# Suffix sums of a stick-breaking attention: matmuls by a matrix of ones, or a reversed scan and transposes, with two heads interleaved

## The chip, the cores and the metric

The kernel runs on one core of one Trainium2 chip. The metric is the device time of one execution in microseconds; the time before is the median of three runs.

## What is computed

The program is a two-block network on 512 tokens of width 2048. The change touches the stick-breaking attention of the first block, 12 heads of 64 columns, handled as 6 pairs. With z the scores of a head, each weight is the sigmoid of its own score times the product of one minus the sigmoids of all later keys that the query may see:

```python
z = jnp.einsum('bhqd,bhkd->bhqk', q[:, :, q0:kend], k[:, :, :kend])
causal = jnp.arange(kend)[None, :] < (q0 + jnp.arange(SB_BLOCK))[:, None]
log_1m = jnp.where(causal, jax.nn.log_sigmoid(-z), 0.0)
after = lax.cumsum(log_1m, axis=3, reverse=True) - log_1m
w = jnp.where(causal, jnp.exp(jax.nn.log_sigmoid(z) + after), 0.0)
outs.append(jnp.einsum('bhqk,bhkd->bhqd', w, v[:, :, :kend]))
```

## The kernel before

The program is one stream of dense projections with everything else laid beside it. A dense product of f32 accuracy takes three matmuls for each 128x128 tile of weights (lines 311 to 313: high parts of weight and activation, then the two cross terms); these three are one **step**. 16 steps make one projection of 128 output columns. The weights arrive in chunks of four tiles (`wr`) and are split by `split_w`: a rounded copy `wh`, written by ScalarE (line 181) or by GpSimd (line 280), and the rest `wl`, subtracted by VectorE (line 163). Which engine copies is counted: in the first pair of heads (`where` 1) GpSimd takes each, in the later pairs (`where` 2) every second one. The split of a chunk is recorded at the second step of a chunk, some three chunks ahead of its use, and each chunk has one of four buffers.

Every engine runs its instructions in the order in which the program records them; nothing is reordered later. So where a helper is recorded sets what stands behind what in each queue. `pump(n)` records the next n steps of the stream. In the attention stage, `Kern.stick`, the stream of pair j is the front of pair j+1: the projections for q, k, v and the gate, 64 steps. Beside the steps it brings at fixed places: the head norms of q and k (`head_rs`: 8 small matmuls at line 383, a Newton iteration for the root on VectorE in `newton`, two broadcast copies at line 392; the matmuls of line 383 stand behind step 41 of a pair, behind step 33 in the first pair since 8 steps are pumped ahead there), 8 transposes at line 406 some steps later, and 4 transposes of v at line 1767 behind step 55. In the first and the last pair of the stage, parts of the pooling group stand in the queues as well. `pump` also draws on a second generator, the parameters of the later S5 layer (small VectorE and GpSimd operations, written out to memory as `s5w`), at .5 of a step's pace in this stage.

One pair runs so before. For each head: 8 score matmuls (line 752, keys on partitions), then on ScalarE abs of the three banks, exp of minus that, and Ln of one plus that (lines 176 and 178, with a table load between), which gives the common part of both log sigmoids in `sbl`. Steps are pumped. VectorE then makes both log sigmoids from scores and `sbl` (lines 1824 and 1825), masks the one that is summed, and splits it into `sbh` and `sbo`. Then for each head the sums over later keys are 20 matmuls against matrices of ones (line 1846), VectorE subtracts them from `sbe`, ScalarE takes the exp, and VectorE masks the weights. The product with v (`values`, line 1791) of a pair is recorded in the next pair. Of the 64 steps, 57 are pumped among these; the rest run in a plain loop at the pair's end. In the last pair the stream is the start of the output projection (`out_ahead`).

Of the kernel before, what the change touches and what calls it, by code (L numbers as in the profile page):

```python
# [9 lines left out]
F32 = mybir.dt.float32  # L10
F32R = mybir.dt.float32r
I32 = mybir.dt.int32
BF16 = mybir.dt.bfloat16
AF = mybir.ActivationFunctionType
OP = mybir.AluOpType
# [4 lines left out]
QOFF = (512, 1024, 640, 0)  # L20
KOFF = (0, 512, 1024, 896)
BANK = ((0, 512), (512, 512), (1024, 256))
# [7 lines left out]
STICK_WAIT = (8,6)  # L30
HEAD_LAG = (3,5,7)
RWKV_STEPS = (0,0,0,(13,6),4,4,3,3,3,1,1)
STICK_STEPS = ((7,7),(9,7),(4,8),(4,11))
EVEN_STEPS = ((3,8),(6,8),10)
ODD_STEPS = ((4,20),16)
LAST_STEPS = ((4,16),14)
# [105 lines left out]
class Kern:  # L142
# [49 lines left out]
    def constants(self, tmp):  # L192
        nc, c = self.nc, self.const
        jp = tmp.tile([128, 128], I32, name="jp")
        nc.gpsimd.iota(jp, pattern=[[1, 128]], base=0, channel_multiplier=-1)
        mk = lambda name: c.tile([128, 128], F32, name=name)
# [23 lines left out]
        mr = lambda name: c.tile([128, 128], F32R, name=name)  # L220
# [3 lines left out]
        V = nc.vector  # L224
# [4 lines left out]
        self.copy(self.ident_r, self.ident)  # L229
        self.one = c.tile([128, 1], F32, name="one")  # L230
        nc.vector.memset(self.one, 1.0)
        self.ones_r = mr("ones_r")
        self.copy(self.ones_r, self.one.to_broadcast([128, 128]))

        self.suf_r = c.tile([128, 128], F32R, name="suf_r")
        nc.vector.tensor_scalar(self.suf_r, jp, 0.0, None, op0=OP.is_lt)

        self.omu = c.tile([128, 25], F32, name="omu")
        o, w = _PV["mu_a"]
        nc.vector.tensor_scalar(self.omu, self.pvt[:, o:o + w], -1.0, 1.0, op0=OP.mult, op1=OP.add)  # L240
        o, w = _PV["k_a"]
# [3 lines left out]
        for n in ("k_a", "a0", "w0", "b_glu_2"):  # L245
            o, w = _PV[n]
# [99 lines left out]

    def pump(self, n):

        for _ in range(n):
            next(self.stream, None)  # L350
            next(self.tail, None)
            self.count += EXTRA_RATE[self.where]
            if self.count >= 1:
                self.count -= 1
                next(self.extra, None)

    def big(self):
        return self.ps.tile([128, 512], F32, name="big", bufs=2)
# [1015 lines left out]
    def rwkv(self, pool, tm, yd, acts, rs):  # L1374
# [105 lines left out]
        for j in range(6):  # L1480
# [4 lines left out]
            if j:  # L1485
                pump(GRAM_WAIT)
# [286 lines left out]

    def causal(self, t):

        d = t.rearrange("p (b n) -> p b n", n=256)[:, 0::2, 0:128]
        self.mul(d, d, self.m_lt[:, None, :].to_broadcast([128, 3, 128]))
        self.mul(t[:, 896:1024], t[:, 896:1024], self.m_lt)

    def stick(self, pool, tm, yd, acts, rs, yl):  # L1780
        nc = self.nc
        V = nc.vector
        OFF = KOFF

        def values(j, vt, W, gate):
            o = self.small()
            for b in range(4):
                n = 512 - 128 * b
                for p in (0, 1):
                    h = slice(64 * p, 64 * p + 64)  # L1790
                    nc.tensor.matmul(o[h, 128 * b:512], vt[:, b, h], W[p][:, OFF[b]:OFF[b] + n],
                                     start=(b == 0), stop=(b == 3))
            self.mul(gate, o, gate)
            if j < 5:
                self.nc.sync.dma_start(yd[SB_AT[j]], gate)

        last = None
        self.second_parts(pool)
        for j in range(6):
            pools = self.pools(6 + j, pool, tm, yd, acts, rs)  # L1800
            self.stream = chain(self.stick_front(tm, j + 1, acts, rs, pool), *pools) if j < 5 else chain(
                *pools, self.out_ahead("w_out", *self.out_operands(yl, yd)))
            q, k, vt, gate = self.ready.pop(j)
            if j == 0:
                q, k = self.stacked_q(pool, q), self.stacked_k(pool, k)
                self.pump(FIRST_STEPS)
            sums = []
            self.where = 2 if j else 1
            for p in (0, 1):
                z = [self.small() for _ in range(3)]  # L1810
                at = lambda b: (z[OFF[b] // 512], OFF[b] % 512)
                for b in (0, 1, 3, 2):
                    t, o = at(b)
                    self.scores(t[:, o:o + 512 - 128 * b], p, slice(128 * b, 512), slice(128 * b, 128 * b + 128), q, k,
                                True)
                N = L = pool.tile([128, 1280], F32, name="sbl", bufs=1)
                E = pool.tile([128, 1280], F32, name="sbe", bufs=3)
                for (o, n), t in zip(BANK, z):
                    self.act(L[:, o:o + n], t[:, 0:n], AF.Abs)
                self.act(L, L, AF.Exp, scale=-1.0)  # L1820
                self.act(L, L, AF.Ln, bias=1.0)
                self.pump(STICK_STEPS[p][0])
                for (o, n), t in zip(BANK, z):
                    V.scalar_tensor_tensor(E[:, o:o + n], t[:, 0:n], 0.0, L[:, o:o + n], op0=OP.min, op1=OP.subtract)
                    V.scalar_tensor_tensor(N[:, o:o + n], t[:, 0:n], 0.0, L[:, o:o + n], op0=OP.max,
                                           op1=OP.add)
                self.causal(N)
                hi = pool.tile([128, 1280], F32R, name="sbh", bufs=2)
                lo = pool.tile([128, 1280], F32R, name="sbo", bufs=2)
                self.split(hi, lo, N)  # L1830
                sums.append((E, hi, lo))
                if last and p == 0:
                    values(*last)
                self.pump(STICK_STEPS[p][1])
            for p, (E, hi, lo) in enumerate(sums):
                s = [self.small() for _ in range(3)]
                for b in (0, 1, 3, 2):
                    t, o = s[OFF[b] // 512], OFF[b] % 512
                    mm = []
                    for b2 in range(b, 4):  # L1840
                        n = 512 - 128 * b2
                        for x in (hi, lo):
                            mm.append((t[:, o + 128 * (b2 - b):o + 128 * (b2 - b) + n],
                                       self.suf_r if b2 == b else self.ones_r, x[:, OFF[b2]:OFF[b2] + n]))
                    for i, (o_, l_, r_) in enumerate(mm):
                        nc.tensor.matmul(o_, l_, r_, start=(i == 0), stop=(i == len(mm) - 1))
                for (o, n), t in zip(BANK, s):
                    self.sub(E[:, o:o + n], E[:, o:o + n], t[:, 0:n])
                self.act(E, E, AF.Exp)
                self.pump(STICK_STEPS[2 + p][0])  # L1850
                self.causal(E)
                self.pump(STICK_STEPS[2 + p][1])
            last = j, vt, [E for E, _, _ in sums], gate
            self.where = 3
            if j == 5:
                self.where = 0
                values(*last)
                self.out_last(gate, "w_out")
            for _ in self.stream:
                pass  # L1860


# [72 lines left out]
```

## Time and profile before

| | |
|---|---|
| median of 3 runs | 3011.6 us (3009.29 to 3014.44) |
| profiled execution, its own time | 3016.27 us |
| its span | 3014.0 us |
| mean granted TensorE clock | 0.98 |
| TensorE busy | 2944.0 us, 98% |
| VectorE busy | 1619.1 us, 54% |
| ScalarE busy | 1146.2 us, 38% |
| GpSimd busy | 373.5 us, 12% |
| attention stage, first score matmul to the end of the last pair | about 602 to 973 us |

TensorE is busy nearly throughout, so what TensorE executes and the few places where it stands idle add up to the time. The other engines' shares are means over the program; what matters of them is whether a result is there when TensorE reaches the instruction that reads it.

### The profile page before, as it was taken

Reading aid. Unit: us, or ns where it says so; the run is one execution under the profiler, and the core shown is the slowest. Engines: PE = TensorE matmul, PEld = TensorE weight load, DVE = VectorE, ACT = ScalarE, POOL = GpSimd, SP = SyncE. Lnnn points to the kernel's source line nnn. Section 1 sums busy time; section 2 is a strip of 40 time slices with the busy share of each in tenths; the row PEclk is TensorE's granted clock in tenths of the full one; section 3 lists DMA queues with packets and bytes.
Section 4 is the critical chain, followed back from the end, with each engine's and each line's share of the span. In section 5 each row is a group of like instructions: output and inputs, shape, how many; then the busy total and the mean of one; then the engine's idle time right before and its main releaser. Section 6 shows DMA issues by size and latency. Waiting matters only on the chain. (4 is left out here: it accounts for less than half of the span.)

```text
span 3014.0 us, 42793 instructions
## 1 busy us (share of the span) xinstructions
PE 2944.0 (98%) x16068; PEld 2418.0 (80%) x16068; DVE 1619.1 (54%) x3253; ACT 1146.2 (38%) x2062; POOL 373.5 (12%) x819
## 2 busy tenths in 40 slices
PE   8999999999999999999999999999999999999998
PEld 6777777778887887788888887888888888888887
DVE  6655555477767675555454455354444444444534
ACT  5443443354454223223344454233333232333432
POOL 0111111013764000211100000001101010100001
PEclk9998999999999999999999999999999999999999
DMA  4211111222234555454433325543332333223443
GB/s 156 67 56 59 57 57 59 78 81 85 94 96 158 158 182 180 135 159 157 138 105 104 102 85 177 146 130 109 101 105 96 98 96 96 95 91 95 148 121 119
DMA packets 195296, 334.01 MB, mean 111 GB/s; under 512 B 29696, under 2 KB 44672, under 8 KB 193936
## 3 DMA queue, kind: packets, MB, share of 16 engines
q1 hardware_dynamic: 193808, 327.08, 34.9%
q0 software_dynamic: 1280, 4.20, 0.4%
q8 instruction: 126, 2.06, 0.3%
q14 instruction: 82, 0.67, 0.1%
HBM read 289.55 MB, written 42.70 MB: 110 GB/s over the span
## 5 line engine op out<-in xcount | busy, mean ns | idle before, releaser
L311 PE MATMUL big<-hi,wh 128*128 128x512 f32 x3424 | 1375.5, 402 | 4.6 <-ACT hi L181 3.9
L312 PE MATMUL big<-lo,wh 128*128 128x512 f32 x3424 | 1347.5, 394 | 2.3 <-DVE lo L163 2.3
L313 PE MATMUL big<-hi,wl 128*128 128x512 f32 x3424 | 1347.0, 393 | 0.7 <-DVE wl L163 0.6
L163 DVE TENSOR_TENSOR wl<-wr,wh 128x512 fp32r<-128x512 f32 x884 | 621.9, 714 | 709.9 <-ACT wh L181 707.6
L311 PEld LDWEIGHTS big<-hi,wh 128*128 128x128 f32 x3424 | 650.1, 190 | 150.2 <-issue 11.1
L181 ACT ACTIVATE wh<-wr 128x512 fp32r<-128x512 f32 x835 | 515.6, 626 | 657.1 <-PE big L312 520.2
L313 PEld LDWEIGHTS big<-hi,wl 128*128 128x128 f32 x3424 | 649.6, 190 | 141.2 <-DVE wl L163 2.7
L312 PEld LDWEIGHTS big<-lo,wh 128*128 128x128 f32 x3424 | 650.8, 190 | 132.8 <-DVE lo L163 5.6
L683 ACT ACTIVATE pm<-pm,mx 128x128 f32<-128x128 f32 (+3 forms) x128 | 70.5, 551 | 178.6 <-DVE mx L679 178.6
L1235 POOL TENSOR_SCALAR dm<-cb,cq 128x128 f32<-128x128 f32 (+1 forms) x64 | 42.4, 663 | 598.4 <-DVE mx L677 580.1
L163 DVE TENSOR_TENSOR tm<-big,rs 128x512 f32<-128x512 f32 x85 | 58.5, 689 | 73.8 <-PE big L313 73.7
L176 ACT ACTIVATE sq<-xn 128x512 f32<-128x512 f32 (+1 forms) x47 | 28.8, 614 | 161.5 <-DVE xn L163 161.5
L181 ACT ACTIVATE pt<-sm 128x512 f32<-128x512 f32 (+3 forms) x96 | 43.4, 526 | 62.7 <-PE sm L711 62.7
L163 DVE TENSOR_TENSOR xn<-big,xr 128x512 f32<-128x512 f32 (+1 forms) x50 | 33.3, 667 | 53.2 <-PE big L313 46.3
L181 ACT ACTIVATE qk<-tm 128x512 fp32r<-128x512 f32 x32 | 20.2, 633 | 96.3 <-DVE tm L163 48.2
L1615 POOL MEMSET xi<- 64x16 f32 x6 | 0.7, 119 | 448.0 <-DVE xi L1614 448.0
L280 POOL CAST wh<-wr 128x512 fp32r<-128x512 f32 x49 | 34.2, 698 | 128.3 <-PE big L312 81.7
L163 DVE TENSOR_TENSOR pl<-sm,pt 128x512 fp32r<-128x512 f32 (+1 forms) x48 | 25.9, 596 | 44.3 <-ACT pt L181 44.3
L689 DVE TENSOR_SCALAR pm<-pm,sm 128x128 f32<-128x128 f32 (+3 forms) x128 | 43.3, 400 | 1.1
L163 POOL TENSOR_TENSOR xn<-xn,rs 128x256 f32<-128x256 f32 x12 | 8.6, 756 | 284.0 <-ACT rs L181 284.0
L1371 DVE SCALAR_TENSOR_TENSOR tm<-big,rs 128x512 f32<-128x512 f32 x33 | 22.7, 689 | 36.5 <-PE big L313 36.5
L311 PE MATMUL sm<-hi,wh 128*128 128x512 f32 x80 | 32.6, 408 | 8.7 <-ACT wh L181 8.7
(449 smaller groups left out, 3118.2 us busy)
## 6 DMA issues: line engine op xcount, KB each, us to landing
wr<-w_in_odd SPq DMA_DIRECT2D x256, 256.0 KB, 3.3
wr<-w_in SPq DMA_DIRECT2D x228, 256.0 KB, 3.1
wr<-w_in_even SPq DMA_DIRECT2D x192, 256.0 KB, 3.5
wr<-w_out SPq DMA_DIRECT2D x64, 256.0 KB, 3.8
wr<-w_out_even SPq DMA_DIRECT2D x64, 256.0 KB, 3.5
wr<-w_out_odd SPq DMA_DIRECT2D x64, 256.0 KB, 3.4
xr<-x SPq DMA_DIRECT2D x48, 256.0 KB, 3.0
yl<-y SPq DMA_DIRECT2D x45, 256.0 KB, 4.2
```

What stands on the lines that cost most here:

```text
L163: (eng or self.nc.vector).tensor_tensor(out, a, b, op=op)
L176: self.nc.scalar.activation(out, x, f, scale=scale)
L181: self.nc.scalar.activation(out, x, AF.Copy, scale=scale)
L280: self.nc.gpsimd.tensor_copy(wh, wr)
L311: nc.tensor.matmul(ps, wh[:, i], hi, start=(k == 0), stop=False)
L312: nc.tensor.matmul(ps, wh[:, i], lo, start=False, stop=False)
L313: nc.tensor.matmul(ps, wl[:, i], hi, start=False, stop=(k == n - 1))
L683: nc.scalar.activation(d, d, AF.Exp, bias=mx[:, b:b + 1], accum_out=sm[:, b:b + 1])
L689: V.tensor_scalar(d, d, sm[:, b:b + 1], None, op0=OP.mult)
L1235: nc.gpsimd.tensor_scalar(D[:, QOFF[b]:QOFF[b] + n], cb[:, 0:n], -1.0, cq[:, b, h:h + 1], op0=OP.mult, op1=OP.add)
L1371: self.nc.vector.scalar_tensor_tensor(t, ps, scale, rs, op0=OP.mult, op1=OP.mult)
L1615: G.memset(X.rearrange("p i c -> p (i c)")[:, 0:256:17], 1.0)
```

## The change

Scores are laid out with queries on partitions (`qblocks`), so that the sum over later keys runs along a row. The 20 matmuls of each head, the split into `sbh` and `sbo` and the subtraction from PSUM are gone. In their place VectorE runs one scan over the reversed row of 1280 columns (`later`; `rows` holds ones, with zeros where a new query block begins) and one subtraction of 1279 columns. After exp and mask, `keys` turns the weights back to keys on partitions: 10 transposes on TensorE (line 711) and three copies by ScalarE into `sbw`. The two heads' parts are interleaved over 46 steps by a new table. The remaining 18 steps of a pair now run through `pump` too, so that the S5 parameters advance with them.

```diff
-STICK_STEPS = ((7,7),(9,7),(4,8),(4,11))
+STICK_STEPS = (8,5,3,6,4,5,2,6,4,3)
...
-        self.ones_r = mr("ones_r")
-        self.copy(self.ones_r, self.one.to_broadcast([128, 128]))
-
-        self.suf_r = c.tile([128, 128], F32R, name="suf_r")
-        nc.vector.tensor_scalar(self.suf_r, jp, 0.0, None, op0=OP.is_lt)
+
+        self.m_gt = mk("m_gt")
+        nc.vector.tensor_scalar(self.m_gt, jp, 0.0, None, op0=OP.is_lt)
...
     def pump(self, n):
 
+        more = False
         for _ in range(n):
-            next(self.stream, None)
+            more = next(self.stream, self) is not self
...
+        return more
...
     def causal(self, t):
 
-        d = t.rearrange("p (b n) -> p b n", n=256)[:, 0::2, 0:128]
-        self.mul(d, d, self.m_lt[:, None, :].to_broadcast([128, 3, 128]))
-        self.mul(t[:, 896:1024], t[:, 896:1024], self.m_lt)
+        m = self.m_gt[:, None, :].to_broadcast([128, 2, 128])
+        d = t[:, 384:640].rearrange("p (b n) -> p b n", n=128)
+        self.mul(d, d, m)
+        d = t[:, 768:1280].rearrange("p (b n) -> p b n", n=256)[:, :, 128:256]
+        self.mul(d, d, m)
...
+        self.rows = pool.tile([128, 1280], BF16, name="rows", bufs=1)
+        V.memset(self.rows, 1.0)
+        for b in range(4):
+            o = 1279 - (QOFF[b] + 128 * b + 127)
+            V.memset(self.rows[:, o:o + 1], 0.0)
...
+            def logits(p):
+
+                z = self.qblocks()
+                for b in (3, 0, 2, 1):
+                    t, o, n = z[b]
+                    self.scores(t[:, o:o + n], p, slice(128 * b, 128 * b + 128), slice(0, n), q, k, False)
+                z = [z[3][0], z[0][0], z[1][0]]
+                N = pool.tile([128, 1280], F32, name="sbl", bufs=2)
                 for (o, n), t in zip(BANK, z):
-                    self.act(L[:, o:o + n], t[:, 0:n], AF.Abs)
-                self.act(L, L, AF.Exp, scale=-1.0)
-                self.act(L, L, AF.Ln, bias=1.0)
-                self.pump(STICK_STEPS[p][0])
+                    self.act(N[:, o:o + n], t[:, 0:n], AF.Abs)
+                self.act(N, N, AF.Exp, scale=-1.0)
+                self.act(N, N, AF.Ln, bias=1.0)
...
+            def later(p):
+
+                _, N, E = heads[p]
+                V.tensor_tensor_scan(N[:, ::-1], self.rows, N[:, ::-1], 0.0, OP.mult, OP.add)
+                self.sub(E[:, 0:1279], E[:, 0:1279], N[:, 1:1280])
+
+            def weights(p):
+                self.act(heads[p][2], heads[p][2], AF.Exp)
+
+            def keys(p):
+
+                W.append(pool.tile([128, 1280], F32, name="sbw", bufs=3))
+                self.turn(heads[p][2], W[p])
+
+            n = iter(STICK_STEPS)
+            logits(0)
+            self.pump(next(n))
+            both(0)
+            if last:
+                values(*last)
+            self.pump(next(n))
+            logits(1)
+            self.pump(next(n))
+            later(0)
+            self.pump(next(n))
+            both(1)
+            self.pump(next(n))
+            weights(0)
+            self.pump(next(n))
+            self.causal(heads[0][2])
+            later(1)
+            self.pump(next(n))
+            keys(0)
+            self.pump(next(n))
+            weights(1)
+            self.pump(next(n))
+            self.causal(heads[1][2])
+            self.pump(next(n))
+            keys(1)
...
-            for _ in self.stream:
+            while self.pump(1):
                 pass
```

`both(p)` holds the six VectorE operations of lines 1824 and 1825 and the mask, unchanged in kind; in the changed file they are lines 1836 and 1837, the dense lines are 309 to 311, and the scan is line 1844.

**ScalarE, third pair, the second head's logits.** `sm` is the scores in PSUM, `wr` and `wh` a weight chunk and its rounded copy. Before:

```order
L176 ACTIVATE sbl<-sm 128x512 x2
L176 ACTIVATE sbl<-sm 128x256
L176 ACT_TABLE_LOAD
L176 ACTIVATE sbl<-sbl 128x1280
L178 ACT_TABLE_LOAD
L178 ACTIVATE sbl<-sbl 128x1280
L176 ACTIVATE tm<-tm 128x512
L181 ACTIVATE wh<-wr 128x512
L181 ACTIVATE sbh<-sbl 128x1280
```

Now:

```order
L176 ACTIVATE sbl<-sm 128x512 x2
L176 ACTIVATE sbl<-sm 128x256
L176 ACT_TABLE_LOAD
L176 ACTIVATE sbl<-sbl 128x1280
L178 ACT_TABLE_LOAD
L178 ACTIVATE sbl<-sbl 128x1280
L181 ACTIVATE wh<-wr 128x512
L176 ACTIVATE tm<-tm 128x512
L181 ACTIVATE wh<-wr 128x512
L176 ACT_TABLE_LOAD
L176 ACTIVATE sbe<-sbe 128x1280
```

In both, a weight copy stands behind the whole chain to Ln; the first head's exp of the weights (`sbe`) now follows a little later on the same queue.

**VectorE, third pair, around the first head's sum.** Before, from the split of the first head's summed logs to the second head's log sigmoids:

```order
L163 TENSOR_TENSOR sbo<-sbl,sbh 128x1280
L163 TENSOR_TENSOR RKV<-sm,RKV 128x512
L163 TENSOR_TENSOR wl<-wr,wh 128x512 x2
L163 TENSOR_TENSOR tm<-big,rs 128x512
L163 TENSOR_TENSOR wl<-wr,wh 128x512 x2
L1824 SCALAR_TENSOR_TENSOR sbe<-sm,sbl 128x512
```

Now, in the same place:

```order
L163 TENSOR_TENSOR RKV<-sm,RKV 128x512
L163 TENSOR_TENSOR wl<-wr,wh 128x512 x2
L1844 SCALAR_TENSOR_TENSOR sbl<-rows,sbl 128x1280
L163 TENSOR_TENSOR sbe<-sbe,sbl 128x1279
L163 TENSOR_TENSOR tm<-big,rs 128x512
L163 TENSOR_TENSOR wl<-wr,wh 128x512 x2
L1836 SCALAR_TENSOR_TENSOR sbe<-sm,sbl 128x512
L1837 SCALAR_TENSOR_TENSOR sbl<-sm,sbl 128x512
```

The second `wl` ahead of the scan is the one whose `wh` ScalarE writes behind the second head's Ln. The second head's log sigmoids (eight operations with the masks) stand behind scan and subtraction; behind them two more `wl` and the mask of the first head's weights, which the first head's transposes read.

**VectorE, third pair, ahead of the second head's transposes.** Now:

```order
L416 SCALAR_TENSOR_TENSOR hy<-ht,hy 128x16
L392 COPY tm<-hy 128x512 x2
L163 TENSOR_TENSOR wl<-wr,wh 128x512
L163 TENSOR_TENSOR sbe<-sbe,m_gt 128x256
L163 TENSOR_TENSOR sbe<-sbe,m_gt 128x2x128
L163 TENSOR_TENSOR wl<-wr,wh 128x512
```

The mask of the second head's weights, which the transposes read, stands behind the Newton iteration of the head norms; those start from the matmuls of line 383, five steps of TensorE ahead of the transposes.

## Rows read from the trace of the kernel before

**Rows 1.** Busy time by stretch: us, PE, PEld, DVE, ACT, POOL, granted clock, DMA share, GB/s

```profile
600.00:720.00 120.00, 114.90 (x569) 95.78 (x568) 95.53 (x268) 60.78 (x79) 20.62 (x38) 0.99 0.26 83
720.00:900.00 180.00, 176.94 (x895) 146.09 (x895) 119.95 (x208) 90.03 (x116) 125.91 (x308) 1.00 0.30 94
900.00:960.00 60.00, 59.00 (x283) 46.52 (x280) 47.08 (x76) 25.65 (x41) 35.29 (x75) 1.00 0.41 125
```

**Rows 2.** TensorE's waits, 590 to 975 us: total us, times, longest

```profile
PE pa L1767 <- DVE tm L163: 3.1, 3, 1.2
PE pa L383 <- ACT tm L176: 2.3, 2, 1.8
...
PE pa L406 <- DVE tm L392: 1.9, 1, 1.9
```

**Rows 3.** Timeline of TensorE (start, us, operation), the sum of one head

```profile
625.53 0.40 PE L1846 MATMUL sm<-sbh,suf_r 128*128 128x512 f32 x1
...
628.24 0.44 PE L311 MATMUL big<-hi,wh 128*128 128x512 f32 x1
```

**Rows 4.** Timeline of TensorE, ten transposes by the same helper in a later stage

```profile
1531.76 1.25 PE L711 MATMUL sm<-ident,pm 128*128 128x128 f32 x10
1532.77 0.48 PE L311 MATMUL big<-hi,wh 128*128 128x512 f32 x1
```

**Rows 5.** Timeline of TensorE, sixteen steps without a wait, and one head's scores

```profile
591.17 0.40 PE L312 MATMUL big<-lo,wh 128*128 128x512 f32 x1
...
602.06 0.39 PE L312 MATMUL big<-lo,wh 128*128 128x512 f32 x1
...
730.96 0.39 PE L752 MATMUL sm<-q,k 128*128 128x512 f32 x1
...
732.23 0.40 PE L311 MATMUL big<-hi,wh 128*128 128x512 f32 x1
```

**Rows 6.** Timeline of ScalarE, third pair, second head: abs, Ln, the weight copy behind

```profile
733.06 1.36 ACT L176 ACTIVATE sbl<-sm 128x512 f32<-128x512 f32 x3 [1.27 <-DVE sbo L163]
...
738.32 1.28 ACT L178 ACTIVATE sbl<-sbl 128x1280 f32<-128x1280 f32 x1
...
740.02 0.61 ACT L181 ACTIVATE wh<-wr 128x512 fp32r<-128x512 f32 x1
```

**Rows 7.** Timeline of VectorE, same place: its wait, and the second head's log sigmoids

```profile
740.67 0.69 DVE L163 TENSOR_TENSOR wl<-wr,wh 128x512 fp32r<-128x512 f32 x1 [4.14 <-ACT wh L181]
741.28 0.68 DVE L1824 SCALAR_TENSOR_TENSOR sbe<-sm,sbl 128x512 f32<-128x512 f32 x1
...
744.84 0.76 DVE L163 TENSOR_TENSOR sbl<-sbl,m_lt 128x384 f32<-128x384 f32 x2
```

**Rows 8.** One line each, durations in ns, and groups by line, 600 to 975 us

```profile
L1407 DVE TENSOR_TENSOR_SCAN tm<-reset,tm x6: 1223/1224/1225, 76.0 to 447.4; 128x512 f32<-128x512 bf16 x6
...
L163 DVE TENSOR_TENSOR sbo<-sbl,sbh 128x1280 fp32r<-128x1280 f32 x12 | 18.9, 1578 | 16.7 <-ACT sbh L181 16.7
```

**Rows 9.** Timeline of VectorE: head norms, and a mask beside a busy GpSimd

```profile
755.31 0.18 DVE L1762 TENSOR_SCALAR hm<-pa 128x16 f32<-128x16 f32 x1 [0.66 <-PE pa L383]
...
758.19 0.86 DVE L392 COPY tm<-hy 128x512 f32<-128x512 f32 x2
...
764.04 1.71 DVE L163 TENSOR_TENSOR sbe<-sbe,m_lt 128x384 f32<-128x384 f32 x2
```

**Rows 10.** Timeline of TensorE, the first operation behind two of its longer waits

```profile
970.99 0.50 PE L311 MATMUL big<-hi,wh 128*128 128x512 f32 x1 [2.15 <-ACT hi L181]
...
1199.41 3.75 PE L1140 MATMUL sm<-U,wt 128*128 128x128 f32 x16 [6.06 <-issue]
```

**Rows 11.** Busy time by stretch, as in Rows 1: behind waits of 1.8, 2.15 and 6.06 us

```profile
630.00:636.00 6.00, 4.21 (x28) 3.72 (x27) 5.63 (x14) 2.27 (x4) 0.30 (x1) 1.00 0.17 57
973.50:976.90 3.40, 3.40 (x9) 2.63 (x8) 0.69 (x1) 0.60 (x1) 0.00 (x0) 0.50 0.41 143
1199.40:1205.60 6.20, 6.19 (x23) 5.62 (x24) 4.38 (x7) 2.11 (x5) 1.72 (x3) 0.50 0.78 265
```

More of the change, by code (lines that the diff above doesn't have):

```diff
@@ L1806, in stick @@
                 self.pump(FIRST_STEPS)
-            sums = []
             self.where = 2 if j else 1
[L1809 to L1817, printed above, removed]
-                for (o, n), t in zip(BANK, z):
-                    self.act(L[:, o:o + n], t[:, 0:n], AF.Abs)
-                self.act(L, L, AF.Exp, scale=-1.0)
-                self.act(L, L, AF.Ln, bias=1.0)
-                self.pump(STICK_STEPS[p][0])
+            heads, W = [], []
@@ new lines, in logits @@
+            def logits(p):
[5 more added lines that the diff above has]
+                N = pool.tile([128, 1280], F32, name="sbl", bufs=2)
+                for (o, n), t in zip(BANK, z):
+                    self.act(N[:, o:o + n], t[:, 0:n], AF.Abs)
+                self.act(N, N, AF.Exp, scale=-1.0)
+                self.act(N, N, AF.Ln, bias=1.0)
+                heads.append((z, N, pool.tile([128, 1280], F32, name="sbe", bufs=2)))
@@ L1823, in stick, with both @@
+            def both(p):
+                z, N, E = heads[p]
                 for (o, n), t in zip(BANK, z):
-                    V.scalar_tensor_tensor(E[:, o:o + n], t[:, 0:n], 0.0, L[:, o:o + n], op0=OP.min, op1=OP.subtract)
-                    V.scalar_tensor_tensor(N[:, o:o + n], t[:, 0:n], 0.0, L[:, o:o + n], op0=OP.max,
+                    V.scalar_tensor_tensor(E[:, o:o + n], t[:, 0:n], 0.0, N[:, o:o + n], op0=OP.min, op1=OP.subtract)
+                    V.scalar_tensor_tensor(N[:, o:o + n], t[:, 0:n], 0.0, N[:, o:o + n], op0=OP.max,
@@ L1826, in stick @@
                                            op1=OP.add)
                 self.causal(N)
[L1828 to L1852, printed above, removed]
@@ L1853, in stick @@
-            last = j, vt, [E for E, _, _ in sums], gate
+            def later(p):
[7 more added lines that the diff above has]
+                self.turn(heads[p][2], W[p])
@@ L1854, in stick @@
+            keys(0)
[5 more added lines that the diff above has]
+            keys(1)
+            last = j, vt, W, gate
             self.where = 3
@@ L1856, in stick @@
                 self.where = 0
+                self.pump(3)
                 values(*last)
                 self.out_last(gate, "w_out")
-            for _ in self.stream:
+            while self.pump(1):
                 pass
```

## The prediction

> **What bounds the kernel now.** I read the busy times by stretch first. In the attention stage TensorE works 114.90 of 120 us, then 176.94 of 180 and 59.00 of 60 [rows 1], so matmuls taken out shorten the kernel one to one, and every wait that TensorE gets lengthens it one to one. Next came TensorE's waits in the stage: what there is comes from the side work, 3.1 us at the v transposes, 2.3 at the head norms' matmuls and 1.9 at their spread [rows 2]; none stands at the sums. So there is little to gain but the matmuls, and the question is whether the new chain of the other engines is done when TensorE reaches the transposes. For that I read the timelines of ScalarE and VectorE in a middle pair and set them in the new order of each queue.
>
> **What is taken out.** The sum of a head holds TensorE from 625.53 to the next dense matmul at 628.24, 2.71 us [rows 3]. Ten transposes by the same helper hold it from 1531.76 to 1532.77, 1.01 us [rows 4]. Scores are the same eight matmuls with operands exchanged, so they cost what they did. That saves 1.70 us a head, times 12 heads **20.4 us**. The split of the summed logs and the subtractions go from ScalarE and VectorE, and the copies into `sbw` come; none of them is on TensorE's time, and what they do to the waits is in the chains below. Loss of two constants and gain of one are a few operations at the start, beside weight transfers, nothing.
>
> **A step** is the unit of cover: sixteen of them last from 591.17 to 602.06, so 0.681 us each [rows 5]. A head's scores take 1.27 us (730.96 to 732.23) [rows 5].
>
> **The first head's transposes (step 33 of a pair).** Count from the second head's first score matmul. Until the transposes TensorE has its scores, 1.27 us, and 3+6+4+5+2 = 20 steps, 13.6 us: 14.9 us of cover. The chain against it: the first bank of scores is there after some 0.75 us (my estimate, over half of the 1.27). ScalarE's abs, exp and Ln with both table loads run from 733.06 to 738.32 + 1.28 = 739.60, 6.54 us; the weight copy behind it takes 0.6 [rows 6]. In the new order of VectorE the `wl` that reads this copy stands ahead of the first head's scan. The first head's sums are ready long before, but the scan is queued behind it. In the kernel before the same `wl` already kept VectorE idle for 4.14 us [rows 7]; it cost TensorE nothing, since only the second head's log sigmoids stood behind it. So VectorE starts that `wl` at 0.75 + 6.54 + 0.6 = 7.9 us. Then:
>
> - `wl`, 0.65 (0.69 in the row, starts 0.61 apart) [rows 7]: 8.55
> - the scan of 1280 columns. No row has it. The scan of 512 columns took 1224 ns [rows 8]. Scaled by columns that is 3.06 us, the upper bound; the lower is an ordinary operation of two inputs over 1280 columns, 1.58 us [rows 8]. I take 2.9, near the scan's own row, which has the recurrence, less a part of its fixed time: 11.45
> - the subtraction over 1279 columns, at most the 1.58 us of the like operation [rows 8]; I take 1.45, since the next may start before its end: 12.9
> - `tm` 0.6 and two `wl` of 0.65, with 0.5 of waiting for ScalarE's square and copy between: 15.3
> - the second head's log sigmoids, 741.28 to 744.84, 3.56 us, and masks 0.72 (0.76 there) [rows 7]: 19.6
> - two `wl`, 1.3, and the mask of the first head's weights, 0.72: 21.6
>
> So the chain needs 21.6 us against 14.9 us of cover, and TensorE waits **6.7 us**. A part of it will appear a step or two earlier, at the dense matmuls whose `wl` is queued behind the same work; it is the same wait.
>
> **The second head's transposes (step 46).** The mask ahead of them stands behind the head norms, whose matmuls (line 383) stand at step 41. From their result VectorE runs from 755.31 to 758.19 + 0.86 = 759.05, 3.74 us [rows 9], then one `wl`, 0.65, and the mask, 0.72: 5.1 us, against five steps, 3.4. TensorE waits **1.7 us**. The scan of the second head, its subtraction and ScalarE's exp run under the eight steps ahead of line 383.
>
> **All pairs.** 8.4 us a pair, times 6, is 50.4 us. VectorE has 39.98 us of work per 60 us in the middle pairs (119.95 over 180), but 15.6 us more in the first 120 us and 7.1 more in the last 60 [rows 1]: S5 parameters and pooling, 22.7 us that stand in the same queue. The two chains span about half of a pair's steps, and some of this work falls into idle time of VectorE, so I take 0.4 of it, 9.1 us (none of it to all: 0 to 22.7). New waits: **59.5 us**.
>
> **What goes.** TensorE's 7.3 us of waits at the v transposes, the head norms and their spread [rows 2] come behind, or within, the new waits, in which the other engines catch up. The waits at the start of the output projection stay, 2.15 us the longest of them [rows 10]. The 18 drained steps of each pair now advance the S5 parameters: 33 advances a pair in place of 28.5, on VectorE and GpSimd behind step 46, where nothing but the next pair's first operands waits; I cost it at nothing, and if it delays the v transposes, it gives back part of their 3.1 us.
>
> **The clock.** Behind a wait of 1.8 us the granted clock stayed at 1.00; behind 2.15 us it was 0.50 (1.2 of 2.4 GHz) for 3.4 us, and behind 6.06 us for 6.2 us [rows 10, 11]. Half of such a stretch is lost: 1.7 and 3.1 us. The wait at the first head's transposes lies between, and its pieces may be apart, so I take the lower, 1.7 us times 6, **10.2 us**; bounds 0 and 18.6. The Trainium skill (TensorE: Matmul & The Clock Gate, What's actually happening) says that the default state is throttled, and activity releases the throttle. By that the sum keeps this term, without it the time is the second rival's; the trace agrees at 2.15 and 6.06 us, and at 1.8 us shows no fall.
>
> **Sum.** -20.4 - 7.3 + 59.5 + 10.2 = +42.0 us. The profiled execution took 3016.3 us (span 3014.0), which would become 3058.3; it is 4.7 us over the median of the three runs shown, 3011.6, and against that the change gives 3053.6, **3054 us**.
>
> **Rivals.**
> 1. *The scan isn't held (faster).* If the rounded copy that VectorE waits for were there before the second head's Ln, as where GpSimd writes it, scan and subtraction would run under ScalarE's chain. The second head's log sigmoids would then begin at about 7.4 us, and the mask would be done at 7.4 + 3.6 + 0.7 + 1.3 + 0.7 = 13.7, inside the 14.9. Left are 1.7 us a pair and up to 9.1: 3011.6 - 27.7 + 10.2 + 9.1 = 3003 us, or 2994 if the extra work is hidden too. It decides at 27.7 / 6 = 4.6 us of wait a pair. For it: TensorE has no wait at the sums before. Against it: the 4.14 us that VectorE stood idle for ScalarE at just this place [rows 7], and the new queue, in which the scan is behind it.
> 2. *The clock stays full.* The wait comes in pieces, none long enough: 3054 - 10 = 3043 us. For it, the stretch behind 1.8 us [rows 11].
> 3. *VectorE's operations are longer than their rows.* The mask took 1.71 us beside a busy GpSimd in place of 0.76 [rows 7, 9], and GpSimd is busy 126 of 180 us here [rows 1]. Three masks in the chains at 0.95 more are 2.9 us a pair, over four pairs 11: 3065 us; a reversed scan at half the forward one's pace would add 2.9 a pair, 17 us: 3071. The Trainium skill (Advanced Engine Details and Errata, GPSIMD Details) says that GpSimd shares a read and a write interface with VectorE and conflicts with operations of two SBUF inputs. That is the case of the mask, of `wl` and of the subtraction; here the row of 1.71 us agrees, while the mean of the 1280-column operation, 1.58 us, leaves little room for it.
> 4. *In between.* The scan runs at the ordinary pace, 1.3 us less a head, the extra work is hidden and the clock stays: 3054 - 10 - 9 - 8 = 3027 us, and down to no change if ScalarE's chain is shorter than in the row.
>
> **Chances.** My forecast .45, the full clock .22, longer operations .16, in between .08, the scan not held .09. What is measured can tell 0.2%, 6 us, from no change. Faster .10 (the first rival and a little of the fourth), same .04 (half of the fourth), slower .86. The range reaches from 3014, low in the fourth case, to 3074, above both prices of the third with a clock that costs a little more; it leaves out the first.
>
> **What would show it.** In the profile after: TensorE's waits name the transposes (line 711) from the mask, and dense lines from `wl`, some 60 us in the stage, and no wait of 3 us at the v transposes; a scan of 2.9 us; VectorE idle some 4 us in each pair ahead of the `wl` before the first scan, released by ScalarE's copy; the sum's lines gone and TensorE's busy time at full clock 20 us less; stretches of granted clock 0.50 behind the first head's transposes. It is wrong if the scan starts ahead of the second head's Ln, or if TensorE's new waits are below 27.7 us.

## The result, and the profile after

The changed kernel takes 3052.5 us (median of 4 runs, 3048.15 to 3055.37) beside 3012.3 us for the kernel before in the same comparison: a ratio of 1.0133, 95% interval 1.0115 to 1.0151, **40 us slower**. The profiled execution took 3055.4 us, its span 3053.5.

The time is added in the attention stage and its tail. From the stage's first score matmul to the first matmul of the S5 layer behind it (line 1140) it was 602.52 to 1199.41 before and is 603.53 to 1239.0 now: 596.9 and 635.5 us, 38.6 more. TensorE's waits in the stage, after (engine, line and releaser, then total us, times, longest; compare [rows 2]):

```profile
PE sm L711 <- DVE sbe L163: 28.8, 12, 5.5
PE big L311 <- DVE wl L163: 16.2, 5, 5.5
PE big L309 <- ACT hi L181: 2.1, 1, 2.1
PE pa L383 <- ACT tm L176: 1.2, 1, 1.2
```

The waits at the v transposes (line 1767) and the spread (line 406) are gone; in their place stand 28.8 us at the new transposes and 16.2 us at dense matmuls whose `wl` is late. The busy times by stretch, columns as in [rows 1], tell the second half:

```profile
600.00:720.00 120.00, 103.39 (x471) 83.99 (x470) 91.91 (x249) 56.57 (x77) 21.75 (x44) 0.90 0.22 74
720.00:900.00 180.00, 159.16 (x742) 127.07 (x741) 119.34 (x179) 83.24 (x116) 127.82 (x296) 0.94 0.27 87
900.00:960.00 60.00, 51.26 (x245) 41.24 (x244) 34.82 (x58) 28.07 (x43) 34.28 (x70) 0.96 0.23 75
...
764.00:770.00 6.00, 3.65 (x13) 3.05 (x14) 6.00 (x5) 0.00 (x0) 5.76 (x6) 0.50 0.25 87
829.00:835.00 6.00, 4.43 (x16) 3.98 (x17) 5.96 (x7) 0.00 (x0) 2.97 (x6) 0.50 0.60 176
```

TensorE works 103 of 120 us where it worked 115, and the granted clock is 0.90 to 0.96 where it was 0.99 to 1.00; in the two short stretches, at the first transposes of the third and fourth pair, it is 0.50. Summed over the trace's record of the clock, the stage had 6.8 us at 0.50 before and 58.0 us after, of which 11.4 are waits. Half of the rest is lost: 3.4 us before, 23.3 after.

The third pair shows the mechanism. The second head's first score matmul starts at 743.85. VectorE from there (start, us, operation, and in brackets the idle time before it; compare [rows 7]):

```profile
744.46 0.68 DVE L163 TENSOR_TENSOR wl<-wr,wh 128x512 fp32r<-128x512 f32 x1
751.67 0.69 DVE L163 TENSOR_TENSOR wl<-wr,wh 128x512 fp32r<-128x512 f32 x1 [6.54 <-ACT wh L181]
752.28 2.83 DVE L1844 TENSOR_TENSOR_SCAN sbl<-rows,sbl 128x1280 f32<-128x1280 bf16 x1
755.15 1.88 DVE L163 TENSOR_TENSOR sbe<-sbe,sbl 128x1279 f32<-128x1279 f32 x1
...
765.52 1.43 DVE L163 TENSOR_TENSOR sbe<-sbe,m_gt 128x256 f32<-128x256 f32 x2
```

ScalarE ahead of that wait (Ln, then the weight copy; compare [rows 6]):

```profile
749.85 1.27 ACT L178 ACTIVATE sbl<-sbl 128x1280 f32<-128x1280 f32 x1
751.03 0.62 ACT L181 ACTIVATE wh<-wr 128x512 fp32r<-128x512 f32 x1
```

And TensorE, same place (the last row is cut off behind seven of the ten transposes):

```profile
758.28 0.50 PE L311 MATMUL big<-hi,wl 128*128 128x512 f32 x1 [2.31 <-DVE wl L163]
...
766.34 1.99 PE L711 MATMUL sm<-ident,sbe 128*128 128x128 f32 x7 [4.81 <-DVE sbe L163]
```

VectorE stands idle 6.54 us with the first head's scan queued behind a `wl`, whose copy ScalarE writes behind the second head's Ln. It starts the `wl` 7.8 us after the first score matmul, the scan 8.4 us, and TensorE gets to its transposes after 22.5 us, having waited 2.31 + 4.81 = 7.1 us.

### The profile page after: what moved, and what is told of

It is laid out like the page before. It is cut to its first block, busy times and chain, and to the rows that moved or that the text cites. A ratio compares the mean times of both kernels' runs of the same rounds, so it can differ in the third digit from the quotient of the medians.

```text
span 3053.5 us, 42536 instructions
## 1 busy us (share of the span) xinstructions
PE 2940.5 (96%) x15948; PEld 2407.3 (79%) x15948; DVE 1634.6 (54%) x3234; ACT 1152.7 (38%) x2093; POOL 377.4 (12%) x811
## 3 DMA queue, kind: packets, MB, share of 16 engines
q0 software_dynamic: 1280, 4.20, 0.4%
## 5 line engine op out<-in xcount | busy, mean ns | idle before, releaser
L311 PE MATMUL big<-hi,wl 128*128 128x512 f32 x3424 | 1351.9, 395 | 16.3 <-DVE wl L163 16.2
L311 PEld LDWEIGHTS big<-hi,wl 128*128 128x128 f32 x3424 | 652.2, 190 | 159.6 <-DVE wl L163 19.8
L176 ACT ACTIVATE sq<-xn 128x512 f32<-128x512 f32 (+1 forms) x47 | 28.8, 613 | 162.0 <-DVE xn L163 162.0
L176 ACT ACTIVATE tm<-tm 128x512 f32<-128x512 f32 (+1 forms) x35 | 22.1, 631 | 113.4 <-DVE tm L163 87.0
L181 ACT ACTIVATE qk<-tm 128x512 fp32r<-128x512 f32 x32 | 20.2, 633 | 96.2 <-DVE tm L163 48.1
L711 PE MATMUL sm<-ident,sbe 128*128 128x128 f32 x120 | 22.9, 349 | 28.9 <-DVE sbe L163 28.8
L711 PEld LDWEIGHTS sm<-ident,sbe 128*128 128x128 f32 x120 | 17.7, 177 | 35.2 <-issue 24.0
```

The lines of the kernel that those rows point to most:

```text
L176: self.nc.scalar.activation(out, x, f, scale=scale)
L181: self.nc.scalar.activation(out, x, AF.Copy, scale=scale)
L311: nc.tensor.matmul(ps, wl[:, i], hi, start=False, stop=(k == n - 1))
L711: nc.tensor.transpose(ps[o // 512][:, o % 512:o % 512 + 128], Pm[:, QOFF[b] + 128 * kb:QOFF[b] + 128 * kb + 128], self.ident)
```

## The experiments

Every run was compared with the kernel before on the same chip, whose median went from 3006.7 to 3012.3 us between the comparisons; so the ratio to it is what counts, and "us more than before" below is that ratio less one, times 3010.

**Is the scan held, or is VectorE overloaded?** Two ways to free the scan. First, the two copying engines exchange their turns from the second pair on, so that GpSimd writes the copy at that place:

```diff
             self.where = 2 if j else 1
+            if j == 1:
+                self.turns += 1
```

> From the second pair on, the turns of the two copying engines are exchanged, so that GpSimd writes the weight copy whose wl stands ahead of the first head's scan, and ScalarE's copy behind the second head's Ln is read only behind the scan and its subtraction. Theory A (the scan is held by the copy queued behind ScalarE's Ln): scan and subtraction run under ScalarE's chain, 4.3 us less on the chain to the first transposes, the wait there with the one at the dense matmuls before it falls from about 7 us to 0.5 to 3 in pairs 2 to 6, and the clock falls less often: 3052 - 5 x 4 - about 8 = 3015 to 3035 us. Rival B (VectorE has too much work in this stretch whatever its order): the waits only move, within 5 us of 3052.

Measured: 3034.1 us, ratio 1.0071 [1.0054, 1.0089], 21 us more than before where the change was 40. In the third pair the second head's first score matmul is at 732.34, and the scan starts 3.0 us behind it, where it was 8.4:

```profile
735.31 2.81 DVE L1846 TENSOR_TENSOR_SCAN sbl<-rows,sbl 128x1280 f32<-128x1280 bf16 x1
```

Second, the scan is recorded earlier:

```diff
             both(0)
+            later(0)
             if last:
                 values(*last)
...
-            later(0)
```

> The first head's scan and subtraction are recorded right behind its log sigmoids, ahead of the product with v and the second head's scores; nothing else moves. Theory A: they no longer stand behind the held wl; 4.4 us less on the chain, waits at the first transposes of about 2.5 us in place of 7, in all six pairs: 3052 - 6 x 4.4 - 6 to 12 of clock = 3012 to 3022 us. The scan takes its 2.8 us all the same. Rival B (volume of VectorE's work): within 5 us of 3052, waits elsewhere. Rival C (the scan itself, with no cover, is the price): within 5 us too, the wait moving to the second head's scores or to wl ahead of them.

Measured: 3034.0 us, ratio 1.0069 [1.0054, 1.0084], again 21 us more than before. VectorE in the third pair of this run, then TensorE's largest wait in the stage:

```profile
745.10 0.69 DVE L163 TENSOR_TENSOR wl<-wr,wh 128x512 fp32r<-128x512 f32 x1 [2.17 <-ACT wh L181]
```

```profile
PE sm L711 <- DVE sbe L163: 31.2, 12, 6.2
```

The idle time ahead of the same `wl` is 2.17 us in place of 6.54: scan and subtraction, 4.3 us, run in it. The work of VectorE is the same, so its volume alone is not what held TensorE; rival B falls. Of 40 us about 19 hung on the place of one operation in a queue. Both runs stayed at the upper end of what was expected or above: waits of 2 to 7 us at the first transposes remain, in the second run 20.2 us over the six pairs, the pieces at dense matmuls included. In its third pair the second head's log sigmoids start at 748.56, 11.3 us behind the first score matmul at 737.27, since three `wl` and a `tm` stand ahead of them in VectorE's queue.

**What does the scan itself cost?** It is replaced by an ordinary product:

```diff
-                V.tensor_tensor_scan(N[:, ::-1], self.rows, N[:, ::-1], 0.0, OP.mult, OP.add)
+                self.mul(N, N, N)
```

> The scan is replaced by an ordinary product over the same 1280 columns (so the sums over later keys are left out; all else runs as before). It measures the scan's price: an ordinary operation of that size takes about 1.55 us in this trace, the scan 2.82. Theory A (the chain to the first transposes carries the wait): the chain is 1.25 us shorter in each pair, 6 x 1.25 = 7.5 us, and 0 to 5 us of clock: 3040 to 3046 us. Rival C (the scan is the main price of the change): 20 us or more less.

Measured: 3041.6 us, ratio 1.0110 [1.0088, 1.0133], 33 us more than before, 7 less than the change. The chain's 1.25 us times 6 would be 7.5; the intervals of the two runs overlap, so the size is not sharp, but the 20 us of rival C lie outside them. In the changed kernel the scan took (minimum, median, maximum in ns):

```profile
L1844 DVE TENSOR_TENSOR_SCAN sbl<-rows,sbl x12: 2810/2818/3229, 619.4 to 967.0; 128x1280 f32<-128x1280 bf16 x12
```

**What stands behind the second transposes' wait?** The second head's mask goes ahead of the head norms:

```diff
             weights(1)
+            self.causal(heads[1][2])
             self.pump(next(n))
-            self.causal(heads[1][2])
             self.pump(next(n))
```

> The mask of the second head's weights is recorded right behind their exp, six to ten steps earlier in VectorE's queue, so that it stands ahead of the head norms' Newton iteration; nothing else moves. Theory G (the prediction's: the second transposes wait for the Newton chain, 5.1 us against 3.4 of cover): their waits (5.54, 1.08, 0.55, 1.52 and 3.42 us in the first five pairs, 0.38 in the sixth) fall below 1 us each, and the spread of the norms (line 406) gets little, since it has two more steps: 3052 - 8 to 12 - 0 to 5 of clock = 3035 to 3044 us. Rival H (VectorE is late altogether, the order matters little): the wait goes over to line 406, 3048 to 3056 us.

Measured: 3029.4 us, ratio 1.0076 [1.0052, 1.0100], 23 us more than before, 17 less than the change, the upper end of what was expected. TensorE's two largest waits:

```profile
PE sm L711 <- DVE sbe L163: 17.8, 6, 4.7
PE big L311 <- DVE wl L163: 15.8, 5, 5.5
```

The transposes wait 6 times instead of 12, the first head's alone; 11 us of waits are gone and nothing came at line 406 (rival H falls). So what stood ahead of the mask in VectorE's queue was the cause. In the second to fifth pair that is the Newton iteration, as the prediction had it. In the first pair, which has the longest of these waits in the changed kernel, 5.54 us, it is something else: the norms stand eight steps earlier there, the Newton iteration had ended at 641.8, and the mask stood behind the splits of q and k, which wait for copies by ScalarE. VectorE there, in the changed kernel:

```profile
651.22 0.69 DVE L163 TENSOR_TENSOR kl<-RKV,k 64x512 fp32r<-64x512 f32 x1 [0.62 <-ACT k L181]
...
652.94 0.75 DVE L163 TENSOR_TENSOR sbe<-sbe,m_gt 128x256 f32<-128x256 f32 x2
```

**Would more steps do?** Seven of the drained steps are put ahead of the first transposes:

```diff
-STICK_STEPS = (8,5,3,6,4,5,2,6,4,3)
+STICK_STEPS = (8,5,3,6,4,5,9,6,4,3)
```

> Seven of the 18 steps that were drained at the pair's end are put ahead of the first head's transposes (table 8,5,3,6,4,5,9,6,4,3), 4.8 us of cover for both heads' transposes; no order changes on VectorE or ScalarE but that of those steps' own work. Theory A: the waits at the transposes nearly vanish (28.8 us before, 0 to 6 now), the wait at the dense matmuls of about 2.3 us a pair, on a wl queued behind the same chain, stays, and it is too short for a fall of the clock every time: 3052 - 25 - 10 = 3010 to 3025 us. Rival B (volume): VectorE is late in the next part of the pair instead, the v transposes wait again, 3035 to 3052.

Measured: 3061.2 us, ratio 1.0165 [1.0148, 1.0182], 50 us more than before and slower than the change. The forecast missed. TensorE's waits:

```profile
PE sm L711 <- DVE sbe L163: 21.7, 5, 5.0
PE big L311 <- DVE wl L163: 18.1, 7, 5.4
PE pa L383 <- ACT tm L176: 8.8, 5, 2.9
PE pa L406 <- DVE tm L392: 5.2, 1, 5.2
```

The first transposes no longer wait; all five at line 711 are the second head's, at 4.6 to 5.0 us but for the last of 2.55, since its mask is recorded seven steps later too and now stands behind the use of the head norms, the splits of q and k, in every pair. Steps cover a wait only if what is waited for keeps its place in the other engines' queues.

**The drain.** The old loop at the pair's end:

```diff
-            while self.pump(1):
+            for _ in self.stream:
                 pass
```

> The drained steps run in the plain loop again, so the S5 parameters advance in the 46 steps alone. The prediction costed this part at nothing: 3049 to 3055 us. Rival D (the operations of the S5 parameters in the drain are what delays the next pair's chain or the transposes): 5 to 15 us less.

Measured: 3067.8 us, ratio 1.0183 [1.0166, 1.0200], 55 us more than before, 15 more than the change: neither theory. The writes of the S5 parameters, in this run and then in the changed kernel (first and last start):

```profile
L1022 POOL DMA_DIRECT2D s5w<-fr x8: 587/588/739, 777.6 to 1026.9; - x8
```

```profile
L1022 POOL DMA_DIRECT2D s5w<-fr x8: 587/587/740, 743.6 to 940.4; - x8
```

With 46 steps a pair advancing them instead of 64 they end 86 us later, behind the stage. There SyncE's queue waits for them with a load of x, and TensorE at the end for that load (waits of SyncE, 980 to 1060 us; timeline of TensorE):

```profile
SPq L633 <- DMA s5w<-fr: 22.7, 2, 19.1
```

```profile
1033.79 0.79 PE L309 MATMUL big<-hi,wh 128*128 128x512 f32 x1 [12.37 <-DVE xn L163]
```

So the table of 46 steps needs the drain's advances. The kernel before does not:

```diff
-            for _ in self.stream:
+            while self.pump(1):
                 pass
```

Here too `pump` returns whether the stream goes on.

> The kernel before, with only the other part of the change: the steps left at a pair's end advance the S5 parameters too. The prediction costed this at nothing against the kernel before, where 57 of 64 steps advance them already and all are written out in this stage: within 4 us of the kernel before. Rival D (the drain's parameters are a gain of their own, as taking them away from the changed kernel cost 15 us): 5 to 15 us faster than the kernel before.

Measured: 3008.0 us, ratio 1.0001 [0.9991, 1.0012], no change. The prediction's nothing holds against the kernel before, where 57 steps advance the parameters.

**The clock.** Matmuls nobody reads fill part of the wait:

```diff
+            o = self.small()
+            for _ in range(16):
+                nc.tensor.matmul(o, self.ident_r, acts[0][0], start=True, stop=True)
             keys(0)
```

> Sixteen matmuls of 512 columns, whose result nobody reads, stand ahead of the first transposes of each pair, 3.65 us at full clock, 22 us in all: TensorE works where it waited. Theory E (the waits cost twice, once themselves and once by the clock that falls behind them, some 20 us of the 40): the waits at the first transposes shrink by what the matmuls take, the granted clock falls less often, and in spite of 96 added matmuls the time falls, to 3038 to 3050 us. Rival F (the fall of the clock has little to do with these waits): the clock falls as often, and the time is the same or, where a pair's wait was shorter than the matmuls (pairs 1, 2 and 6), longer, 3052 to 3062 us.

Measured: 3049.0 us, ratio 1.0144 [1.0122, 1.0166], 43 us more than before, not to be told from the change. TensorE's largest waits:

```profile
PE big L311 <- DVE wl L163: 16.2, 5, 5.4
PE sm L711 <- DVE sbe L163: 15.0, 7, 6.6
```

The fall of the time that theory E expected did not show; but 96 matmuls, 21.9 us of work at full clock, cost some 3 us by the ratios, whose intervals overlap, and not 22. By the profile, the stage's waits went from 49.4 to 35.2 us, 14.2 less, its falls of the clock from 11 to 7, and the loss at half clock from 23.3 to 15.2, 8.1 less; together that is 22.3, about what was added. So the falls go with the waits (rival F, the same number of falls, does not fit), and filling a wait with work gives back some of the clock.

**Do saved matmuls shorten the stage one to one?** The kernel before with 12 of 20 matmuls in each sum left out:

```diff
-                    for b2 in range(b, 4):
+                    for b2 in range(b, b + 1):
```

> The kernel before without the 12 of 20 matmuls of each head's sum that add the blocks of later keys (so later blocks are left out of the sums; all else runs). By the timeline of the kernel before they hold TensorE 0.76 + 0.41 + 0.16 = 1.33 us a head, 16.0 us in 12. Theory I (matmuls taken out of this stage shorten it one to one, as the prediction's 20.4 us supposes): 15 to 17 us faster than the kernel before. Rival J (the other engines' chains have no slack left there, and the saving returns as waits): 0 to 10 us faster.

Measured: 3008.0 us, ratio 0.9992 [0.9979, 1.0005]: 16 us of matmuls out, and no gain that can be measured. TensorE's largest waits there, compare [rows 2]:

```profile
PE pa L1767 <- DVE tm L163: 9.7, 4, 2.7
PE sm L1846 <- DVE sbl L1825: 3.6, 5, 1.4
```

The v transposes wait 9.7 us where they waited 3.1, the sums 3.6 where they waited 0.8; all waits of the stage went from 11.7 to 19.8 us, so about half of the 16 us came back as waits. From the first score matmul to line 1140 the profiled run is 592.8 us, 4.1 less than before, a gain that the interval admits. Rival J holds: though TensorE is busy 98%, the chains through ScalarE and VectorE were almost as long as a pair's matmuls already.

**A version that takes this together.** First both moves and a new table, with the second head's exp and mask right behind the first transposes:

```diff
-STICK_STEPS = (8,5,3,6,4,5,2,6,4,3)
+STICK_STEPS = (8,5,9,4,5,7,8)
...
             both(0)
+            later(0)
...
             logits(1)
-            self.pump(next(n))
-            later(0)
             self.pump(next(n))
...
             keys(0)
-            self.pump(next(n))
             weights(1)
-            self.pump(next(n))
             self.causal(heads[1][2])
```

> Both moves together, with the steps put where the chains need them: the scan right behind the first head's log sigmoids, the first transposes at step 38 in place of 33 (3.4 us more cover), the exp and mask of the second head's weights right behind them, the second transposes at step 46 as before. Theory A and G: chain to the first transposes 17.3 us against 18.3 of cover, the mask of the second head ahead of the norms; waits of 0 to 1.5 us a pair in pairs 3 to 5, some more in 1, 2 and 6, 10 to 20 us in all with the 3 at the stage's end; clock loss under 8: 3012 - 20 + 0 to 15 = 2990 to 3010 us. Rival B (volume): 3025 or more.

Measured: 3012.5 us, ratio 1.0018 [1.0006, 1.0029], 5 us more than before where 2 to 22 less was expected. The transposes no longer wait (0.7 us); the largest wait is now

```profile
PE pa L383 <- ACT tm L176: 9.8, 5, 2.4
```

the head norms' square, whose VectorE product stood behind the second scan. So that scan is recorded two steps later:

```diff
             self.causal(heads[0][2])
+            self.pump(next(n))
             later(1)
...
-STICK_STEPS = (8,5,9,4,5,7,8)
+STICK_STEPS = (8,5,9,4,5,2,5,8)
```

> As the run with reordered steps, but the second head's scan and subtraction are recorded two steps later, behind the VectorE product that the head norms' square on ScalarE reads. There TensorE's longest waits were at the head norms' matmuls (line 383), 9.8 us in five pairs, each followed by 3.4 us at half clock. Theory A (order in VectorE's queue): the product is done 4.4 us earlier, these waits vanish but in the first pair, with the fall of the clock behind them: 7.4 + 4 x 1.7 = 14 us less than that run (3012 us there, beside 3007 for the kernel before): 2996 to 3003 us, faster than the kernel before. Rival B (volume): the wait goes over to the spread of the norms (line 406) or the second transposes, 3007 to 3014.

Measured: 3010.5 us, ratio 1.0000 [0.9985, 1.0015], so the gain over the kernel before that was expected did not come. The waits at line 383 vanished but in the first pair, as expected, but waits for a weight copy on GpSimd grew from 2.4 to 7.1 us:

```profile
PE big L309 <- POOL wh L278: 7.1, 2, 4.1
PE big L311 <- DVE wl L163: 4.5, 4, 1.8
```

GpSimd ahead of the longer one:

```profile
803.37 0.54 POOL L1022 DMA_DIRECT2D s5w<-fi  x1
805.19 0.10 POOL L1010 MEMSET fr<- 128x4 f32 x1 [1.28 <-DMA s5w<-fr]
806.01 0.10 POOL L1011 MEMSET fi<- 128x4 f32 x1 [0.71 <-DMA s5w<-fi]
...
806.36 0.60 POOL L278 CAST wh<-wr 128x512 fp32r<-128x512 f32 x1
```

The copy takes 0.60 us but stands behind the S5 parameters' writes and the release of their buffers. The last run lets ScalarE write all copies from the second pair on:

```diff
-POOL_SPLITS = {1:1,2:2}
+POOL_SPLITS = {1:1}
```

> As the run before it (later behind the norms' square), but from the second pair on ScalarE writes all weight copies. There TensorE waited 7.1 us in two pieces for copies on GpSimd, which stood behind the S5 parameters' products and the release of their buffers by DMA. Theory K (GpSimd's queue is what holds those copies): these waits go with the fall of the clock behind them, 7.1 + 5 us; ScalarE has 8 copies of 0.6 us more in each pair, behind its exp and Ln at two places: the waits for wl (4.5 us) grow by 0 to 6. 2994 to 3004 us beside 3009 for the kernel before, faster than it. Rival L (ScalarE's chain is the next limit): more than 8 us of new waits for wl, 3007 to 3020.

Measured: 2995.7 us, ratio 0.9955 [0.9940, 0.9969], **13.5 us faster than the kernel before**, as theory K has it, and 54 faster than the change as made. TensorE's largest waits in the stage:

```profile
PE big L309 <- ACT hi L181: 3.4, 1, 3.4
PE big L311 <- DVE wl L163: 3.2, 2, 2.4
PE pa L383 <- ACT tm L176: 2.3, 1, 2.3
PE pa L1767 <- DVE tm L163: 2.3, 2, 1.8
```

No wait is left in the third and fourth pair. From the first score matmul to line 1140 it is 581.6 us, 15.3 less than before. How much of the gain is the copies' new engine alone was not tried on the kernel before.

## Why the prediction was right

The forecast was 3054 us, the measurement is 3052.5. The mechanism of the first transposes and its place are the ones forecast. That the numbers agree within 2 us is luck: the sum had the new waits 14.5 us too large, the clock 9.7 too small and the saving of matmuls 1.4 to 3 too large; only the 7.3 us of old waits that go came out as forecast.

- **Matmuls, -20.4 us.** By the profile: 38.6 us longer, less 37.7 of waits (49.4 against 11.7) and 19.9 of clock in the stage, leaves -19.0. With waits and clock both taken up to line 1140, where they rose by 37.9 and 18.2 us, it is -17.4. The 1.01 us for ten transposes holds where nothing disturbs them, as in 7 of 12 cases of the last version and at the end of the changed kernel's stage (rows below). Where the missing 1.4 to 3 us lie was not found.

```profile
976.94 1.25 PE L711 MATMUL sm<-ident,sbe 128*128 128x128 f32 x10
977.95 0.48 PE L309 MATMUL big<-hi,wh 128*128 128x512 f32 x1
```

- **First transposes, 6.7 us a pair.** In the third and fourth pair they waited 7.1 and 6.6 us, the piece at the dense matmuls included; in the first pair, where GpSimd writes each copy, 2.2. The chain was forecast to start VectorE's `wl` at 7.9 us (7.8), the scan at 8.55 (8.4) and to end at 21.6 (22.5). The scan's 2.9 us was 2.82, the subtraction's 1.45 was 1.6. VectorE's idle time ahead of that `wl`, forecast as some 4 us, was 5.7 to 7.3 us in the second to sixth pair.
- **Second transposes, 1.7 us.** 1.1, 0.55, 1.5 and 3.4 us in the second to fifth pair, behind the Newton iteration, none in the sixth. The 5.5 us of the first pair had another cause, the splits of q and k, which the prediction did not have there; so the sum of 12.1 us is near the forecast's 10.2 in part by luck.
- **New waits in all, 59.5 us: mis-sized.** They were 28.8 + 16.2 = 45.0. The first transposes had 32.9 us in place of 40.2, since the first, fifth and sixth pair waited less than the middle ones. The 9.1 us for the additional VectorE work in the first and last pairs did not come (first pair 7.7 us, last 5.8, against 8.4 in the forecast without it). That half clock lengthens the steps behind a wait (dense matmuls start 0.43 us apart at 638 us, 0.23 at 600), and so covers part of the next, would also lower them; this was not tried apart.
- **The clock, 10.2 us: mis-sized.** 19.9, above the upper bound of 18.6. The step took one fall a pair of 3.4 us; there were 11 in the stage, 6 of them of 6.8 us, two or three in some pairs. Rival 2 (the clock stays full) falls with them.
- **The drain, nothing:** right against the kernel before, as its run with the parameters in the drain shows; the step did not see that without it the new table would be 15 us slower, as the run with the plain drain shows. The diff shown above the prediction leaves out one more line, three steps pumped ahead of the last pair's product with v; TensorE has no wait there.
- **Rivals.** The scan that isn't held (3003 us) became real only when it was moved, and then gave 3034. Its sum had the second transposes, but no wait at the first ones and no clock. In the run with the scan recorded earlier the first transposes still waited 20.2 us, as the second head's log sigmoids began at 11.3 us (third pair) and not at 7.4, and the loss at half clock in the stage was 17.3. The third rival's lengthening is there, smaller than its 2.9 us a pair: beside a GpSimd that was busy 5.76 of 6 us (764 to 770) the pair of masks took 1.43 us against 0.76 [rows 7], and the scan's longest is 3.23 beside a median of 2.82. The subtraction took 1.88 us in the third pair and 1.49 in the first, where GpSimd did nothing beside it. That GpSimd is the cause was not tried apart.

One premise of the prediction fell: that matmuls taken out of this stage shorten it one to one. The sum came out all the same, as it counted the new chains' waits apart. The run with 12 of 20 matmuls left out shows that the kernel before had little slack in the other engines' chains; the 20 us had to be bought with their time.

## What to carry to other kernels

Before an operation is put on a busy engine's queue, look at what stands ahead of it there and what that waits for: the scan cost 2.8 us and was held 6.5 us by a weight split that waited for another engine's table functions. A busy share of 98% does not say that less matmul work is less time; take some out and see where the waits come back. And add the clock to each new wait where it falls behind it: here 37.7 us of waits came with 19.9 us more lost at half clock.

## What was not expected of the hardware

A wait of 1.79 us in the profile of the kernel before was followed by a granted clock of 1.00 [rows 11]. In the run of the kernel before with the parameters in the drain, TensorE waited 1.80 us at the same place, up to 625.77, and the clock behind it was 0.50 (us, busy times, granted clock as in [rows 1]):

```profile
625.80:632.00 6.20, 6.20 (x19) 5.23 (x20) 5.68 (x25) 4.12 (x5) 0.65 (x1) 0.50 0.30 86
```

Nor is it this place alone. In the kernel before the clock was 0.50 at 697 us, behind a wait of only 0.56 us up to 695.20; in the changed kernel it was 1.00 behind the wait of 2.31 us up to 758.28, and fell within the next wait, of 4.81 us. The first row is of the kernel before, the second of the changed one:

```profile
697.00:700.40 3.40, 3.40 (x15) 3.20 (x13) 3.02 (x16) 0.00 (x0) 0.00 (x0) 0.50 0.34 114
758.30:761.40 3.10, 3.10 (x13) 2.34 (x13) 2.52 (x4) 3.07 (x4) 2.61 (x10) 1.00 0.37 133
```

So the length of the wait alone does not decide at this size, and rival 2's evidence, one such wait, was weak. What else decides was not tried.
